# Plain units on whole banks: 512 tokens past each weight tile, four banks instead of three

## The chip, the cores and the metric

One Trainium2 chip, one of its cores. The metric is the device time of one execution in microseconds, the median over several runs; lower is better. The kernel before runs in 2796.94 us (three runs, 2796.71 to 2799.17).

## What is computed

One layer of a hybrid block over 512 tokens of 2048 features, in float32, followed by a final RMSNorm. Cut to what matters here:

```python
h = rmsnorm(x, norm1_w)
proj = h @ w_in                               # [512, 2048] x [2048, 22592]
q, k, v, g_ret, z, xbc, dt_raw, gate_r, gate_s = split(proj)
y_r = retention(q, k, v, positions) * silu(g_ret)          # 8 heads of 256
y_s = rmsnorm(ssd(xbc, dt_raw, ...) * silu(z), ssd_norm_w) # 4096 wide
merged = sigmoid(gate_r) * (y_r @ w_br_ret) + sigmoid(gate_s) * (y_s @ w_br_ssd)
out = rmsnorm(x + merged @ w_out, norm_f_w)
```

Nearly all of the arithmetic is in products of a weight matrix with 2048 features of 512 tokens: 88 blocks of 256 weight columns of `w_in`, 8 of `w_br_ret`, 16 of `w_br_ssd` (two halves of its 4096 rows) and 8 of `w_out`.

## The kernel before, in words

**Units.** `unit` (line 239) makes W^T A for 256 columns of weights and all 512 tokens, feature-major, as two tiles of 128 x 512. It goes through 2048 features in eight pairs of 128-row tiles (`k` in `products`, line 207). Operands of a matmul are F32R, which rounds, so that each product is three matmuls on a high and a low part of either side: high x high (L202), high x low (L203) and low x high (L204), each accumulated in the same place of a PSUM bank. A bank holds 512 float32 a partition, and every matmul here streams 256 of them: one half of the tokens or of a combination of such halves.

**Two recipes.** A pair of weight tiles times a pair of activation tiles is a 2 x 2 block product, with the token halves as the second dimension. `SEVEN` (line 92) is Strassen's product in Winograd's form: seven products of combinations, four banks, 7 x 3 = 21 matmuls for a `k`. `EIGHT` (line 95), for units called with `plain=True`, is the usual eight products on the weights as they are, 24 matmuls for a `k`, in three banks; it spares VectorE the combining of weights (lines 219 to 222) and makes four weight slots instead of seven to split (line 226). The activations are kept once for both recipes, as seven slots of 256 tokens for each `k` and part (`hh`, `hl`; `operands`, line 162), among them A11 (slot 1), A22 (2), A12 (3) and the difference A21 - A11 (6). There is no slot with A21 itself in it. So `EIGHT` puts the products with A11 into bank 0 for both halves of the outputs and adds those with A21 - A11 into banks 1 and 2.

**Which units are plain.** 18 of the 119 units: V and K of head 0, the first x unit of each of the 8 SSD groups (`PLAIN_X`), the last gate unit, units 0 and 7 of each of the three branch projections and unit 0 of the output projection (`PLAIN2`). The last 256 output columns are a case of their own (`PASSES`, line 99), which the change leaves alone. Three of the 18, the units 7 of the branch projections, take their banks from the `att` pool (`alt`); the other 15 have the `acc` banks `pb0` to `pb2`, which have one buffer each, so that the next unit writes a bank only when it has been read out.

**Order in a unit.** For the first five `k` all products of a `k` follow each other; the last three (`LAST`) are taken group by group (lines 234 to 237), so that a bank is complete, and can be read out, while the later groups still run. In `EIGHT` the groups of the last three `k` are 18, 27 and 27 matmuls long.

**Reading out.** A plain unit's banks are read by three instructions (lines 250 to 253): ScalarE copies bank 0 twice over (for each output column tile once) into the 128 x 1024 result `o`, and VectorE adds bank 1 to one half of `o` and bank 2 to the other.

**Weights.** SP issues the loads of raw weights `wf` (line 216), two `k` in a buffer, three buffers; VectorE combines them for `SEVEN`; ScalarE rounds them to `whi` (line 150, seven buffers) and VectorE subtracts for `wlo` (line 151, six buffers). At the start of a stage the same two lines, with lines 155 to 160 on VectorE and POOL, make the operands `hh` and `hl` of the new stage's activations from DRAM. These have one buffer each, so that they wait for the last matmuls of the stage before.

**Order of issue.** The tile framework puts every engine's instructions in an order by priority and by a timing model of its own (`schedule_with_timeline_sim`, line 819); weight preparation and reading out have a raised priority. Some stretches (stage 0, the end) are pinned to the order of the text by `InOrder`, so that their instructions all have line 120.

Of the kernel before, what the change touches and what calls it, by code (L numbers as in the profile page):

```python
# [8 lines left out]
F32 = mybir.dt.float32  # L9
# [3 lines left out]
ALU = mybir.AluOpType  # L13
PSUM = bass.MemoryType.PSUM
DRAM = bass.MemoryType.DRAM
# [16 lines left out]

# columns of the constant array
C_ID, C_TRI, C_ONE, C_FREQ, C_END = 0, 128, 256, 384, 386


def _parts_of_inverse_two_pi():
    """1/(2 pi) as a sum of 12-bit pieces, high to low."""
    digits = 0.15915494309189533576888376337251436203445964574045644874766734405889
    from fractions import Fraction  # L40

    # 1/(2 pi) to 200 bits by Machin's formula
    def atan_inv(n, bits):
        one = 1 << bits
        term = one // n
        total, k, sign = term, 1, 1
        while term:
            term //= n * n
            k += 2
            sign = -sign  # L50
            total += sign * (term // k)
        return total

    bits = 240
    pi = 4 * (4 * atan_inv(5, bits) - atan_inv(239, bits))
    inv = Fraction(1 << bits, 2 * pi)
    assert abs(float(inv) - digits) < 1e-15
    parts = []
    for i in range(5):
        step = Fraction(1, 1 << (14 + 12 * i))  # L60
        n = inv // step
        parts.append(float(n * step))
        inv -= n * step
    return parts


def constants():
# [7 lines left out]
    for h in range(NH):  # L75
# [5 lines left out]

# A 256-row by 256-column block of weights B times a 256-feature by 512-token block of
# activations A.  Rows of A are the token halves, its columns the two feature tiles; t1 is
# half 1 and t0 is half 2, the odd weight tile is column 1 and the even one column 2.
# Activation slots: 0 A21, then A12-(A21+A22-A11), 1 A11, 2 A22, 3 A12, 4 A21+A22,
# 5 A21+A22-A11, 6 A21-A11.
# Weight slots: 0 B12, then B22+B11-B12, 1 B11, 2 B22, 3 B21, 4 B11-B12, 5 B22-B12,
# 6 B21-(B22+B11-B12).
# A product is (bank, half of the bank, weight slot, activation slot).
# SEVEN: Strassen's products in Winograd's form.  EIGHT: the block product with A21 as  # L90
# A11+(A21-A11), on the weights as they are.
SEVEN = (((0, 0, 1, 1), (1, 0, 3, 3), (1, 1, 0, 5)),
         ((2, 0, 5, 6), (2, 1, 4, 4)),
         ((3, 0, 6, 2), (3, 1, 2, 0)))
EIGHT = (((0, 0, 1, 1), (0, 1, 0, 1)),
         ((1, 0, 1, 6), (1, 0, 3, 2), (1, 1, 3, 3)),
         ((2, 0, 0, 6), (2, 0, 2, 2), (2, 1, 2, 3)))
# EIGHT in two passes, the second half of the tokens first, each with banks of its own.
PASSES = ((((0, 0, 1, 1), (0, 1, 0, 1)), ((1, 0, 3, 3), (1, 1, 2, 3))),
# [12 lines left out]
class InOrder:  # L112
    """An engine whose instructions issue in the order of the program."""

# [15 lines left out]
def hybrid_block(tc, A, out):  # L130
# [15 lines left out]
    def att_tile():  # L146
        return att.tile([P, T], F32, name="att")
# [4 lines left out]

    # ------------------------------------------------ products with the weights
    def combined(f, eng):
# [7 lines left out]
    def operands(i, f):  # L162
        """The seven activation operands of feature pair i from its raw slots 0-3 in f."""
        combined(f, POOL if i in FORM_POOL else DVE)
# [12 lines left out]
    def load_operands(forms, src, last=None):  # L177
        """Operands of 2048 features of a DRAM array [features, T]; the last pair may be on chip."""
        H = []
# [9 lines left out]
    def products(H, parts, pt, groups, PE=PE, after=None):  # L189
        """The products of groups, for 256 columns of weights, into the banks pt: parts are  # L190
        DRAM arrays [2048, n], side by side."""
        started, ws = set(), []
# [46 lines left out]
    def unit(H, parts, alt=False, plain=False):  # L239
        """W^T A for 256 columns of weights as two tiles [128, T], feature-major."""  # L240
        nb = 3 if plain else 4
        if alt:
            pt = [att_tile().rearrange("p (h t) -> p h t", h=2) for b in range(nb)]
        else:
            pt = [acc.tile([P, 2, 256], F32, name=f"pb{b}") for b in range(nb)]
        products(H, parts, pt, EIGHT if plain else SEVEN)
        o = op.tile([P, 4, 256], F32, name="o")
        with tc.high_priority():
            if plain:
                ACT.copy(o.rearrange("p (c r) t -> p c r t", c=2),  # L250
                         pt[0][:, :, None, :].to_broadcast([P, 2, 2, 256]))
                DVE.tensor_tensor(o[:, 0:2, :], pt[1], o[:, 0:2, :], op=ALU.add)
                DVE.tensor_tensor(o[:, 2:4, :], pt[2], o[:, 2:4, :], op=ALU.add)
            else:
# [8 lines left out]

    # ---------------------------------------------------------------- stage 0
    cc = cst.tile([P, C_END], F32, name="cc")
# [8 lines left out]

    # scratch
    yr_d = dp.tile([D, T], F32, name="yr_d")
# [12 lines left out]
    def inverse_root(dst, ps, y, z, n, DVE=DVE, ACT=ACT):  # L289
        """dst = (ps / n + eps) ** -0.5 for sums in PSUM; a Newton step makes it exact.  # L290
        y, z: room for one tile each."""
        ACT.activation(y, ps, AF.Abs_reciprocal_sqrt, scale=1.0 / n, bias=eps)
# [4 lines left out]

    # forms of the activations before they are split: A8 and B8 serve other ends between
    bg_ctx = ExitStack()
# [15 lines left out]
    with tc.tile_pool(name="st0", bufs=1) as st:  # L315
        def early(tag):
            """Room of an operand that is not yet there."""
            return hp.tile([P, 7 * 256], F32, name=f"e_{tag}", tag=tag)

        # the order of the arithmetic here is that of the text  # L320
        pe, act, dve, pool = (InOrder(tc, e) for e in (PE, ACT, DVE, POOL))
        raw = [early(f"hl{i}")[:, :2 * T].rearrange("p (r t) -> p r t", r=2) for i in range(NP)]
        wdt = early("hh7")[:, :KD * SH].rearrange("p (k c) -> p k c", k=KD)
        for i, x in enumerate(raw):
            SP.dma_start(out=x, in_=rows(A["xT"], i))
            if i == 0:
                SP.dma_start(out=cc, in_=A["consts"])
        # brings the table in ahead
        act.activation(rstd[:, :1], eps, AF.Abs_reciprocal_sqrt)
# [27 lines left out]

        # the normalized activations
        fs, hs, H = {}, {}, []
# [25 lines left out]
    def rotary_tables(positions, x):  # L385
        """cos and sin of the angles, which are rounded as the reference rounds them, then
        counted in turns and reduced exactly; x is room for four tiles."""
        turn, a1, a2, ki = (x[:, i, :] for i in range(4))
# [34 lines left out]
    def step_sizes(v, pool):  # L423
        """dt = softplus(h w + bias), the cumulative decays in blocks of 128 tokens."""
        u, w, s, s2 = (v[:, i, :].rearrange("p (c h) -> p c h", c=TB) for i in range(4))
# [8 lines left out]
        for tb in range(TB):  # L434
            DVE.scalar_tensor_tensor(u[:, tb, :], pt[:, tb * SH:(tb + 1) * SH], rstd[:, tb:tb + 1], dtb,
                                     op0=ALU.mult, op1=ALU.add)
        # softplus: max(u, 0) + log1p(exp(-|u|)), log1p(w) = 2 atanh(w / (2 + w))
        DVE.tensor_scalar(w, u, -1.0, None, op0=ALU.mult)
# [36 lines left out]

    # -------------------------------------------------------------- retention
    with tc.tile_pool(name="ret", bufs=1) as rp:
# [3 lines left out]
        for h in range(NH):  # L481
            # the decays stay where the gate comes later
            dec = sg[:, 0, :]
# [72 lines left out]

    # -------------------------------------------------------------------- SSD
    with tc.tile_pool(name="ssd", bufs=1) as sp:
        # conv taps and bias; D
        cw = sp.tile([P, 48, 5], F32, name="cw")  # L560
# [12 lines left out]
        def conv(x, j, dst):  # L573
            """causal convolution over tokens and SiLU of one feature block."""
            ACT.activation(dst, x, AF.Identity, scale=cw[:, j, 3:4], bias=cw[:, j, 4:5])
# [13 lines left out]
        for g in range(NG):  # L589
# [14 lines left out]
            for jj in range(2):  # L604
# [5 lines left out]
                for e in range(2):  # L610
# [5 lines left out]
                    for i in range(2):  # L616
                        SP.dma_start(out=E[i * 64:(i + 1) * 64, :], in_=E_d[h0 + i, P:].partition_broadcast(64))
                    # x token-major, scaled by dt, and by dt and the decay to the block's end
                    ps = att_tile()
# [21 lines left out]
                    for i in range(2):  # L641
                        # decay from s to l within a block; s > l is zeroed by CB
                        L = sp.tile([P, TB, P], F32, name="L", bufs=2)
# [28 lines left out]

    # --------------------------------------------------- branch projections
    with tc.tile_pool(name="br", bufs=1) as bp:
# [41 lines left out]

    # ----------------------------------------------------- output projection
    with tc.tile_pool(name="fin", bufs=1) as fp:
# [16 lines left out]

        # the last two feature blocks, the odd one first, half of the tokens after the other
        t = xo[NP - 1]
# [85 lines left out]
```

## Time and profile before

| | |
|---|---|
| Time, median of 3 runs | 2796.94 us |
| Span of the profiled execution, first to last instruction | 2798.7 us |
| TensorE (PE) busy | 2738.8 us, 98%, 22236 matmuls |
| Weight loads (PEld) busy | 2680.0 us, 96% |
| VectorE (DVE) busy | 2380.8 us, 85% |
| ScalarE (ACT) busy | 1333.9 us, 48% |
| POOL busy | 254.1 us, 9% |
| Mean granted TensorE clock | 0.993 |
| DMA, mean | 130 GB/s |

The profiled execution has only its span as its own time; it lies 1.8 us above the median of the runs and within their spread (2796.71 to 2799.17). The profile names a helper's line, so that the matmuls of all units stand under L202 to L204, those of `acc` banks with the tile `pb` and those of `att` banks with `att`; weight loads stand beside them as PEld. An instruction's duration on PE reaches over the pipeline and is longer than the distance from one start to the next; it is the distance that tells how fast the engine goes.

### The profile page before, as it was taken

The page shows a single profiled execution, that of the slowest core. Times are in us where ns is not written, and L with a number is a line of the kernel's source. Part 1 is how long each engine was busy: PE and PEld are TensorE (multiplying, and loading weights), DVE is VectorE, ACT ScalarE, POOL GpSimd, SP SyncE. Part 2 cuts the span into 40 slices and gives each one's busy share as a digit, 9 for nine tenths or more (in the row PEclk, how much of TensorE's full clock was granted, in tenths as well). Part 3 has the DMA queues.
Part 4 walks back from the last instruction along what each step waited for, and adds up shares of the span by engine and source line. Part 5 has one row for each costly group of instructions (what it writes and reads, how often), then busy time and mean ns, then how long its engine had stood idle before and what let it go on. Part 6 is the DMA issues. An engine that isn't in the chain of part 4 may idle for free.

```text
span 2798.7 us, 55732 instructions
## 1 busy us (share of the span) xinstructions
PE 2738.8 (98%) x22236; PEld 2680.0 (96%) x22236; DVE 2380.8 (85%) x3746; ACT 1333.9 (48%) x1885; POOL 254.1 (9%) x206
## 2 busy tenths in 40 slices
PE   7999999999999999999999999999999999999898
PEld 4999999999999999999999999999999999999898
DVE  8998888888879888888888888888888798788997
ACT  4434333333345655564655555555553343433443
POOL 4000000000000000000000000000020030111311
PEclk9999999999999999999999999999999999999999
DMA  3333333333333444343443434334455554566634
GB/s 124 106 97 101 102 102 103 110 92 109 102 104 119 127 134 127 108 137 108 127 125 121 135 121 135 104 118 128 124 187 165 167 180 130 166 184 190 220 105 139
DMA packets 344388, 362.69 MB, mean 130 GB/s; under 512 B 25664, under 2 KB 298304, under 8 KB 344128
## 3 DMA queue, kind: packets, MB, share of 16 engines
q1 hardware_dynamic: 323888, 325.32, 38.5%
q10 hardware_dynamic: 20240, 33.82, 3.3%
q8 instruction: 174, 2.85, 0.4%
q14 instruction: 86, 0.70, 0.1%
HBM read 321.56 MB, written 37.49 MB: 128 GB/s over the span
## 4 chain that ended last, share of the span: by engine, by line
PE 82%; DVE 7%; DMA 6%; issue 3%; POOL 1%; ACT 1%; SPq 0%; DVEq 0%; ACTq 0%; POOLq 0%
PE pb L203 22%; PE pb L202 22%; PE pb L204 22%; PE att L204 2%; PE att L202 2%; PE att L203 2%; PE att L651 2%; DVE wlo L151 2%; DMA wf<-in_w_in_dram 2%; PE att L537 1%; PE att L522 1%; DMA wf<-in_w_br_ssd_dram 1%; PE att L655 1%; PE pb L120 1%; PE att L630 1%
## 5 line engine op out<-in xcount | busy, mean ns | idle before, releaser
L203 PE MATMUL pb<-hl,whi 128*128 128x256 f32 x5944 | 1686.5, 285 | 10.8 <-DVE hl L120 6.0
L202 PE MATMUL pb<-hh,whi 128*128 128x256 f32 x5944 | 1685.7, 285 | 6.2 <-ACT hh L150 3.2
L204 PE MATMUL pb<-hh,wlo 128*128 128x256 f32 x5944 | 1673.5, 284 | 3.7 <-DVE wlo L151 3.6
L150 ACT CAST whi<-wf 128x896 fp32r<-128x896 f32 (+1 forms) x968 | 822.1, 885 | 873.9 <-PE pb L203 414.8
L203 PEld LDWEIGHTS pb<-hl,whi 128*128 128x128 f32 x5944 | 1141.9, 192 | 17.6 <-DVE hl L120 6.9
L202 PEld LDWEIGHTS pb<-hh,whi 128*128 128x128 f32 x5944 | 1139.3, 192 | 10.2 <-ACT hh L150 3.6
L204 PEld LDWEIGHTS pb<-hh,wlo 128*128 128x128 f32 x5944 | 1136.0, 192 | 5.5 <-DVE wlo L151 5.1
L151 DVE TENSOR_TENSOR wlo<-wf,whi 128x896 fp32r<-128x896 f32 (+1 forms) x968 | 997.4, 1040 | 78.6 <-PE pb L204 25.9
L219 DVE TENSOR_TENSOR wf<-wf 128x512 f32<-128x512 f32 x404 | 286.3, 709 | 168.1 <-DMA wf<-in_w_in_dram 114.3
L204 PE MATMUL att<-hh,wlo 128*128 128x256 f32 x864 | 241.8, 285 | 7.8 <-DVE wlo L151 7.8
L202 PE MATMUL att<-hh,whi 128*128 128x256 f32 x864 | 245.4, 285 | 1.4 <-ACT whi L150 1.4
L203 PE MATMUL att<-hl,whi 128*128 128x256 f32 x864 | 244.8, 285 | 0.0
L221 DVE TENSOR_TENSOR wf<-wf 128x256 f32<-128x256 f32 x404 | 182.8, 454 | 4.3
L204 PEld LDWEIGHTS att<-hh,wlo 128*128 128x128 f32 x864 | 165.1, 193 | 8.8 <-DVE wlo L151 8.8
L222 DVE TENSOR_TENSOR wf<-wf 128x256 f32<-128x256 f32 x404 | 170.7, 424 | 3.2
L202 PEld LDWEIGHTS att<-hh,whi 128*128 128x128 f32 x864 | 167.6, 194 | 1.8 <-ACT whi L150 1.6
L203 PEld LDWEIGHTS att<-hl,whi 128*128 128x128 f32 x864 | 167.5, 194 | 0.0
L626 POOL TENSOR_TENSOR xl<-xd,sst 128x384 f32<-128x384 f32 x32 | 33.6, 1049 | 876.9 <-DVE xd L623 819.7
L646 ACT ACTIVATE L<-L,sst 128x128 f32<-128x128 f32 x256 | 80.1, 390 | 59.6 <-DMA L<-A_d 47.1
L256 ACT COPY o<-pb 128x256 f32<-128x256 f32 x89 | 32.9, 370 | 144.4 <-PE pb L204 137.2
L257 DVE TENSOR_TENSOR o<-pb,o 128x512 f32<-128x512 f32 x89 | 60.9, 684 | 34.5 <-PE pb L204 34.2
L543 POOL TENSOR_TENSOR rs<-rs,mhalf 128x1 f32<-128x1 f32 x32 | 24.9, 784 | 709.5 <-DVE rs L542 700.2
(230 smaller groups left out, 2113.1 us busy)
## 6 DMA issues: line engine op xcount, KB each, us to landing
wf<-in_w_in_dram SPq DMA_DIRECT2D x640, 256.0 KB, 3.1
wf<-in_w_br_ssd_dram SPq DMA_DIRECT2D x128, 256.0 KB, 3.6
wf<-in_w_out_dram SPq DMA_DIRECT2D x72, 256.0 KB, 3.2
wf<-in_w_in_dram SPq DMA_DIRECT2D x128, 128.0 KB, 2.6
L<-A_d SPq DMA_DIRECT2D x64, 256.0 KB, 3.5
wf<-in_w_br_ret_dram SPq DMA_DIRECT2D x64, 256.0 KB, 3.7
ys_d<-B ACTq DMA_DIRECT2D x32, 256.0 KB, 2.8
E<-E_d SPq DMA_DIRECT2D x64, 96.0 KB, 3.0
```

The costliest lines, as they stand in the source:

```text
L150: ACT.copy(dst_hi, src)
L151: DVE.tensor_tensor(dst_lo, src, dst_hi.bitcast(F32), op=ALU.subtract)
L202: PE.matmul(o, wh, xh, start=b not in started, stop=False, skip_group_check=True)
L203: PE.matmul(o, wh, xl, start=False, stop=False, skip_group_check=True)
L204: PE.matmul(o, wl, xh, start=False, stop=(k == NP - 1), skip_group_check=True)
L219: DVE.tensor_tensor(f2[:, :, 4:6, :], f2[:, :, 1:3, :], f2[:, :, 0:1, :].to_broadcast([P, 2, 2, P]), op=ALU.subtract)
L221: DVE.tensor_tensor(f2[:, :, 0, :], f2[:, :, 2, :], f2[:, :, 4, :], op=ALU.add)
L222: DVE.tensor_tensor(f2[:, :, 6, :], f2[:, :, 3, :], f2[:, :, 0, :], op=ALU.subtract)
L257: DVE.tensor_tensor(o[:, 1:3, :], pt[1], p1[:, None, :].to_broadcast([P, 2, 256]), op=ALU.add)
L626: POOL.tensor_tensor(xl, xd[:, :TB - 1], tail[:, :TB - 1, hs, None].to_broadcast([P, TB - 1, 2, 64]), op=ALU.mult)
L646: ACT.activation(L[:, c, :], L[:, c, :], AF.Relu, scale=-1.0, bias=At[:, c, h0 + i:h0 + i + 1])
L651: PE.matmul(pi[i * 64:(i + 1) * 64, c * P:(c + 1) * P], xd[:, c, i, :], L[:, c, :], start=True, stop=True)
```

## The change

Plain units take their products from `FOUR` instead of `EIGHT`. A product's half and its activation slot are now slices: `ALL` is both halves of a bank, 512 columns, `A1` the slots 1 and 6 (A11 and A21 - A11), `A2` the neighbouring slots 2 and 3 (A22 and A12). Each of the four weight slots meets each of its activations in one matmul of 512 columns, and has a bank to itself: banks 0 and 1 belong to one output column tile, banks 2 and 3 to the other. So a `k` has 12 matmuls of 512 columns instead of 24 of 256, the same columns in all. `unit` takes four banks for both recipes, and reads out for each output column tile in three steps: ScalarE copies the A11 half of the first bank twice, VectorE adds that bank's other half (256 columns) to the second half of the tokens, then the whole second bank (512 columns). `products` is unchanged, except that its text goes without its docstring, and `SEVEN`, `PASSES` and the lists of plain units stay. The other lines of the diff take out comments and docstrings only.

```diff
-EIGHT = (((0, 0, 1, 1), (0, 1, 0, 1)),
-         ((1, 0, 1, 6), (1, 0, 3, 2), (1, 1, 3, 3)),
-         ((2, 0, 0, 6), (2, 0, 2, 2), (2, 1, 2, 3)))
-# EIGHT in two passes, the second half of the tokens first, each with banks of its own.
+ALL, A1, A2 = slice(0, 2), slice(1, 7, 5), slice(2, 4)
+FOUR = (((0, ALL, 1, A1),), ((1, ALL, 3, A2),), ((2, ALL, 0, A1),), ((3, ALL, 2, A2),))
...
     def unit(H, parts, alt=False, plain=False):
-        """W^T A for 256 columns of weights as two tiles [128, T], feature-major."""
-        nb = 3 if plain else 4
+
         if alt:
-            pt = [att_tile().rearrange("p (h t) -> p h t", h=2) for b in range(nb)]
+            pt = [att_tile().rearrange("p (h t) -> p h t", h=2) for b in range(4)]
         else:
-            pt = [acc.tile([P, 2, 256], F32, name=f"pb{b}") for b in range(nb)]
-        products(H, parts, pt, EIGHT if plain else SEVEN)
+            pt = [acc.tile([P, 2, 256], F32, name=f"pb{b}") for b in range(4)]
+        products(H, parts, pt, FOUR if plain else SEVEN)
         o = op.tile([P, 4, 256], F32, name="o")
         with tc.high_priority():
             if plain:
-                ACT.copy(o.rearrange("p (c r) t -> p c r t", c=2),
-                         pt[0][:, :, None, :].to_broadcast([P, 2, 2, 256]))
-                DVE.tensor_tensor(o[:, 0:2, :], pt[1], o[:, 0:2, :], op=ALU.add)
-                DVE.tensor_tensor(o[:, 2:4, :], pt[2], o[:, 2:4, :], op=ALU.add)
+                for c in range(2):
+                    ACT.copy(o[:, 2 * c:2 * c + 2, :], pt[2 * c][:, 0:1, :].to_broadcast([P, 2, 256]))
+                    DVE.tensor_tensor(o[:, 2 * c, :], pt[2 * c][:, 1, :], o[:, 2 * c, :], op=ALU.add)
+                    DVE.tensor_tensor(o[:, 2 * c:2 * c + 2, :], pt[2 * c + 1], o[:, 2 * c:2 * c + 2, :], op=ALU.add)
```

## Rows read from the trace of the kernel before

**Rows 1.** The page's busy time, share of the span, instructions of each engine.

```profile
PE 2738.8 (98%) x22236; PEld 2680.0 (96%) x22236; DVE 2380.8 (85%) x3746; ACT 1333.9 (48%) x1885; POOL 254.1 (9%) x206
```

**Rows 2.** PE timeline inside a plain x unit: start us, us, instruction.

```profile
1276.75 0.28 PE L202 MATMUL pb<-hh,whi 128*128 128x256 f32 x1
1276.87 0.28 PE L203 MATMUL pb<-hl,whi 128*128 128x256 f32 x1
...
1278.31 0.28 PE L203 MATMUL pb<-hl,whi 128*128 128x256 f32 x1
```

**Rows 3.** PE timeline in a stretch of lower clock, start of the first branch projection.

```profile
2096.72 0.42 PE L202 MATMUL att<-hh,whi 128*128 128x256 f32 x1
...
2097.79 0.41 PE L203 MATMUL att<-hl,whi 128*128 128x256 f32 x1
```

**Rows 4.** Stretches: us, PE, PEld, DVE, ACT, POOL busy (instructions), PEclk, DMA share, GB/s.

```profile
2096.10:2100.00 3.90, 3.88 (x19) 3.87 (x20) 3.90 (x4) 2.41 (x2) 2.36 (x1) 0.56 0.41 124
43.00:76.00 33.00, 26.85 (x195) 25.74 (x196) 31.00 (x31) 15.00 (x14) 19.07 (x13) 0.90 0.15 43
76.00:808.00 732.00, 732.00 (x5826) 714.74 (x5826) 623.58 (x1088) 284.44 (x367) 24.91 (x32) 1.00 0.34 102
808.00:2058.00 1250.00, 1245.52 (x10386) 1229.52 (x10385) 1063.54 (x1688) 707.88 (x1113) 78.03 (x63) 1.00 0.41 123
2081.60:2109.00 27.40, 25.43 (x195) 24.81 (x194) 25.38 (x34) 12.82 (x14) 9.86 (x8) 0.94 0.58 173
2605.00:2640.00 35.00, 26.62 (x204) 26.01 (x203) 32.05 (x42) 16.98 (x18) 12.62 (x10) 0.90 0.41 125
```

**Rows 5.** PE timeline before the first unit: float32 matmuls of 512 and 2 columns.

```profile
40.77 1.45 PE L120 MATMUL att<-e_hl,e_hh 128*64 128x512 f32 x3
42.16 1.05 PE L120 MATMUL att<-cc,R 128*128 128x2 f32 x8
43.07 0.36 PE L202 MATMUL pb<-hh,whi 128*128 128x256 f32 x1
```

**Rows 6.** Who PE waited for, 76 to 2058 us: us in total, times, longest.

```profile
PE att L595 <- ACT A L580: 2.0, 1, 2.0
PE pb L202 <- DVE o L257: 1.0, 1, 1.0
PE pb L204 <- DVE wlo L151: 0.2, 1, 0.2
```

**Rows 7.** The same from 2058 us to the end.

```profile
PE att L204 <- DVE wlo L151: 7.8, 5, 3.3
PE pb L203 <- DVE hl L151: 4.7, 2, 4.5
PE pb L204 <- DVE wlo L151: 3.5, 4, 1.1
PE pb L202 <- ACT hh L150: 3.2, 2, 2.9
```

**Rows 8.** Reading out, by line and shape: busy us, mean ns, idle before and why.

```profile
L250 ACT COPY o<-pb 128x1024 f32<-128x1024 f32 x15 | 15.2, 1014 | 22.0 <-PE pb L204 22.0
L250 ACT COPY o<-att 128x1024 f32<-128x1024 f32 x3 | 3.0, 1001 | 0.0
L252 DVE TENSOR_TENSOR o<-pb,o 128x512 f32<-128x512 f32 x15 | 10.3, 687 | 13.0 <-PE pb L204 13.0
L253 DVE TENSOR_TENSOR o<-pb,o 128x512 f32<-128x512 f32 x15 | 10.2, 682 | 0.0
L259 DVE TENSOR_TENSOR o<-o,pb 128x256 f32<-128x256 f32 x89 | 36.6, 412 | 0.0
L510 ACT ACTIVATE A<-o 128x512 f32<-128x512 f32 x16 | 9.3, 626 | 3.8 <-DVE o L260 3.7
```

**Rows 9.** Who DVE waited for, whole span: us in total, times, longest.

```profile
DVE o L252 <- PE pb L204: 13.0, 10, 2.1
```

## The prediction, made blind

> **What bounds the kernel now.** I read the busy shares first. TensorE is busy for 98% of the span, its weight loads for 96%, VectorE for 85% [rows 1]. A PE duration reaches over the pipeline, so a high share does not yet tell the bound; the list of what PE waited for does. From 76 to 2058 us, over two thirds of the time, its waits come to a handful of microseconds [rows 6]: there the time is the number of matmuls times the distance between two starts. After 2058 us the branch and output projections have real waits, for weights and operands that VectorE and ScalarE make [rows 7]; the first unit of the program waits too, with VectorE busy 31.0 of 33.0 us [rows 4]. So a faster unit pays in full in the middle, and may be taken back by VectorE where a stage begins.
>
> The distance itself is in the timeline. Inside a plain unit 14 matmuls of 256 columns start within 1.56 us, 0.120 us apart [rows 2], at granted clock 1.00, the 2.4 GHz level. 256 columns at one a cycle would take 0.1067. Where the clock was granted at half, after PE had stood idle at the start of a stage, six starts lie 1.07 us apart, 0.214 each [rows 3, 4], and 256 columns at 1.2 GHz are 0.2133. So a column costs one cycle and hardly anything is fixed beside it; yet at full clock 13 ns come from elsewhere. Eight matmuls of 2 columns each take 0.91 us until the next kind starts, 0.114 each [rows 5]: about that is the least that a matmul with a weight load of its own takes, however little it streams. I read the 0.120 as this floor, in sight because 256 columns at full clock are shorter than a load.
>
> **The change part by part.** *Matmuls.* A plain unit has 8 x 24 = 192 matmuls of 256 columns, 192 x 0.120 = 23.04 us. It gets 96 of 512 columns. No row shows such a matmul in F32R. The lower bound is one column a cycle, 0.213; the upper, if the 13 ns stay on every matmul, 0.227, and 0.240 if they belong to the columns. The nearest row for a long stream is the float32 one: three of 512 columns last 1.45 us together, and with 0.59 for the last one's pipeline that is 0.43 from start to start [rows 5], or 2 cycles a column (0.4267) and some 3 ns. I take 0.216, because the half-clock stretch, whose stream is also longer than the load, shows neither 13 ns more (0.227) nor an eighth more (0.240). A unit then takes 96 x 0.216 = 20.74 us, 2.30 less; 18 units (15 and 3 copies of bank 0 [rows 8]), 41.5 us.
>
> The Trainium skill (TensorE: Matmul & The Clock Gate, section Back-to-back issue gap) gives for a single stream N/2.4 + 2.5 ns, 109 ns for 256 columns and 216 for 512. By it a pair of matmuls would win 2.6 ns instead of 24, and the whole change 1728 x 2.6 ns = 4.5 us instead of 41.5. The trace disagrees at 256 columns (120), and so I go by the row.
>
> *Where it counts.* Thirteen of the 18 units stand where PE has next to no wait behind it: K of head 0 (in 76 to 808 us, PE busy throughout), the eight x units and the last gate unit (808 to 2058 us and just beyond), and units 7 of the three branch projections, the last of their stages. These give 13 x 2.30 = 29.9 us. VectorE has the room for it in the long middle stretch: 1063.5 us busy of 1250 [rows 4], 85%, and 1070 of 1232 afterwards, 87%. The other five are the first of a stage: V of head 0 and units 0 of the four projections. In two of them PE is busy for 26.85 of 33 us and 26.62 of 35, VectorE for 31.0 and 32.1 [rows 4]; PE gets operands as VectorE finishes them, and a shorter stream waits longer for the same operand. I count them at nothing; the bounds are 0 and 11.5 us.
>
> *Reading out.* Now ScalarE copies once, 1.01 us, and VectorE adds twice, 0.687 + 0.682 [rows 8]. Afterwards ScalarE copies 512 columns twice, 0.63 each by the nearest 512-column row, 0.24 more a unit at 48% load: nothing. VectorE adds 256 and 512 columns, twice: 2 x (0.412 + 0.682) = 2.19 us, 0.82 more a unit. In the middle stretch the 15% that VectorE is idle hide it. At the four changes of stage from 2058 us on it does not: the last unit's adds stand in VectorE's queue with the operands for which PE is about to wait. I charge 4 x 0.82 = 3.3 us; the bounds are 0 and 14.8 for all 18.
>
> *The fourth bank.* A plain unit first writes bank 3 after 9 matmuls, 1.9 us; the unit before needs one add of 0.68 for it after its own end. The next seven-product unit writes bank 3 after 15 x 0.120 = 1.8 us, against 9 x 0.120 = 1.1 us for bank 2 now, which was the plain unit's last. Neither is tight, and waits for a bank are now single ones of up to 1.0 us [rows 6]: nothing either way. No DMA is added or moved; SP's queue only meets a consumer that is 10% faster in 18 of 119 units.
>
> *Order.* The tile framework works out every engine's order from its own times, which the change alters. No row prices that; I take nothing, and some 6 us to either side.
>
> The sum: 29.9 - 3.3 = 26.6 us. The profiled execution's span of 2798.7 becomes 2772.1; the median lies 1.8 below that span, so 2796.9 becomes **2770.3 us**.
>
> **The rivals.**
> *All 18 units pay.* Operands of a new stage are rounded into buffers that the old stage's last matmuls release, and those come earlier; if VectorE starts that much earlier and the adds hide, it is 41.5 us: 2755.4. For it: at the branch stages PE also finds work in a neighbouring unit while it waits (the matmuls into `att` banks at 2096 us [rows 3] belong to the second unit, while the first, in `pb` banks, is not yet through). Against: VectorE's 32.1 of 35 us at the last change of stage.
> *The 13 ns stay on each matmul.* Then 1.28 us a unit: 13 x 1.28 - 3.3 = 13.3 us, 2783.6. Against it stands the half-clock distance of 0.214.
> *Stage ends are taken back too.* If VectorE or the transfers pace a new stage from before the old one's end, the gate unit and the three units 7 give nothing: 9 x 2.30 - 3.3 = 17.4 us, and longer waits bring another stretch or two of half clock, some 1.5 us each (16 matmuls at 0.214 instead of 0.120): 2782.5. For it: waits of up to 4.5 us [rows 7].
> *Nothing to win in the stream.* The 0.120 is what 256 F32R columns cost at full clock, load or no load; 512 take 0.240, PE gains nothing, and VectorE's 3.3 us are left: 2800.2, no change that can be told. For it: no row has a longer F32R stream. Against: an eighth more per column would make 0.240 of 256 columns at half clock, where the row has 0.214. The skill's rule for the gap, above, ends near this case by another way, at 2792.4.
> *VectorE's queue blocks, and the kernel is slower.* VectorE takes its instructions in order. An add that waits for a bank holds up the weight splits behind it; it did so 10 times before the first add of a plain unit, 13.0 us in all [rows 9]. The new reading out has four adds and more places to wait. If PE then waits for `wlo` once a plain unit as long as the longest such wait now, 3.3 us [rows 7], it is 18 x 3.3 = 59.4 against 29.9: 2826. It decides from 1.7 us a unit (29.9 / 18). Against: in the middle PE waited 0.2 us for `wlo` in all [rows 6], so the splits run well ahead, and a wait there must first eat that lead.
>
> **How the numbers follow.** Forecast 0.58; all units 0.10; 13 ns stay 0.10; stage ends 0.10; nothing 0.04; slower 0.08. The first four are gains beyond 0.2% (5.6 us, about what a measurement of this kernel can tell from no change): faster 0.88, same 0.04, slower 0.08. The range holds these four: from the full 41.5 us with 2 to spare, 2753, to the two weaker ones at 2783.6 with as much, 2786. Its bounds also take in the unknown order (6 us) around the forecast.
>
> **What would show it.** PE should have 20508 matmuls (3456 fewer of 256 columns, 1728 of 512), starts in a plain unit 0.216 us apart, and a plain x unit of 96 x 0.216. From 76 to 2058 us the waits should stay at some microseconds, with VectorE at 87%; the waits after 2058 us and before 76 us should grow by several microseconds, as the five units' 11.5 us turn into waiting. The forecast is wrong in its main term if the distance is 0.227 or 0.240, in its second if the waits at the changes of stage grow by much more than 11 us, and as a whole if waits for `wlo` show up in the SSD stretch behind the x units.

## The result and the profile after

The median goes from 2796.8 us (4 runs of the kernel before, 2794.8 to 2799.2) to 2780.3 us (4 runs, 2777.5 to 2781.3): a ratio of 0.9935, with the interval 0.9921 to 0.9949. Timed anew, beside other kernels, it was 0.9928 (0.9915 to 0.994). In the rest of this text a gain is (1 - ratio) x 2797 us, so 18.2 us here and 20.1 us the second time, where 26.6 were forecast. The sign and the range hold; the size does not. The profiled execution has a span of 2777.6 us, 21.1 less than before.

The page's line of busy time, beside [rows 1]:

```profile
PE 2715.8 (98%) x20508; PEld 2586.4 (93%) x20508; DVE 2391.4 (86%) x3782; ACT 1336.1 (48%) x1905; POOL 253.1 (9%) x206
```

PE has the 20508 matmuls foretold, and the 1728 spared take only 23.0 us off its busy time. The PE timeline in a plain x unit (start us, us, instruction), beside [rows 2], says why:

```profile
1277.65 0.39 PE L204 MATMUL pb<-hh,wlo 128*128 128x512 f32 x1
...
1280.83 0.39 PE L203 MATMUL pb<-hl,whi 128*128 128x512 f32 x1
```

From the first row to the last are 14 distances in 3.18 us, 0.227 each. Of the three prices that the prediction had named for a matmul of 512 columns (0.213 to 0.216, 0.227, 0.240) it is the middle one: twice the 0.1067 of 256 columns, and 13 to 14 ns once for each matmul. A unit saves 96 x 13.3 ns = 1.28 us and not 2.30.

The first matmuls of this x unit, of the unit after it and of the x unit of the next SSD group, before:

```profile
1272.07 0.28 PE L202 MATMUL pb<-hh,whi 128*128 128x256 f32 x1
...
1296.43 0.28 PE L202 MATMUL pb<-hh,whi 128*128 128x256 f32 x1
...
1432.59 0.28 PE L202 MATMUL pb<-hh,whi 128*128 128x256 f32 x1
```

and after:

```profile
1274.45 0.40 PE L202 MATMUL pb<-hh,whi 128*128 128x512 f32 x1
...
1297.64 0.28 PE L202 MATMUL pb<-hh,whi 128*128 128x256 f32 x1
...
1433.09 0.40 PE L202 MATMUL pb<-hh,whi 128*128 128x512 f32 x1
```

The x unit takes 23.19 us, where before it took 24.36: 1.17 less. The whole group takes 158.64 us, where it took 160.52: 1.88 less. The 0.71 us that the x unit does not explain are taken up with `banks_only` below.

The stretches beside [rows 4] (us, then busy of PE, PEld, DVE, ACT, POOL, PEclk, DMA share, GB/s):

```profile
43.00:76.00 33.00, 23.67 (x84) 17.96 (x83) 30.99 (x31) 14.25 (x13) 18.75 (x12) 0.86 0.16 44
808.00:2040.00 1232.00, 1227.50 (x9583) 1183.30 (x9582) 1063.69 (x1699) 707.47 (x1120) 78.91 (x62) 1.00 0.41 125
70.10:76.90 6.80, 5.63 (x13) 4.46 (x14) 6.66 (x8) 2.13 (x2) 0.00 (x0) 0.50 0.54 147
```

In the SSD stretch VectorE works 1063.69 of 1232 us, 86% (87% were foretold), and PE is still busy throughout. From the first matmul of the first x unit to that of the last gate unit it takes 1235.9 us, where it took 1250.1: 14.2 us of the 21.1 come from here. The two matmuls, before and then after:

```profile
808.45 0.28 PE L202 MATMUL pb<-hh,whi 128*128 128x256 f32 x1
...
2058.56 0.28 PE L202 MATMUL pb<-hh,whi 128*128 128x256 f32 x1
```

```profile
810.88 0.40 PE L202 MATMUL pb<-hh,whi 128*128 128x512 f32 x1
...
2046.80 0.40 PE L202 MATMUL pb<-hh,whi 128*128 128x512 f32 x1
```

The first of the eight x units does not gain: it takes 28.8 us, where it took 26.6. PE waits longer for ScalarE in it (3.2 us, where [rows 6] have 2.0), and after this wait the clock is granted at half for 3.4 us, which it was not before. The granted clock of that place (the third number from the right), before and after:

```profile
820.00:840.00 20.00, 18.54 (x156) 18.55 (x157) 15.48 (x23) 11.64 (x15) 0.00 (x0) 1.00 0.23 69
820.00:840.00 20.00, 16.47 (x73) 13.46 (x72) 12.55 (x22) 14.65 (x19) 0.00 (x0) 0.91 0.18 53
```

In the first unit of the program VectorE has no room, 30.99 of 33 us. The second unit starts at 78.6 us, where before it started at 76.0: 2.6 us later, though the first began 1.2 us earlier (41.9 for 43.1), so that from start to start it is 36.7 us for 32.9.

PE's waits from 76 to 2046 us (us in total, times, longest), beside [rows 6]:

```profile
PE att L599 <- ACT A L579: 3.2, 1, 3.2
PE att L654 <- DVE S L636: 0.7, 2, 0.4
PE pb L204 <- DVE wlo L151: 0.3, 1, 0.3
```

and from 2046 us to the end, beside [rows 7]:

```profile
PE pb L202 <- ACT hh L150: 7.1, 2, 6.0
PE pb L204 <- DVE wlo L151: 5.6, 3, 3.3
PE pb L203 <- DVE hl L151: 2.5, 3, 1.2
PE att L204 <- DVE wlo L151: 2.0, 4, 1.3
```

In the middle PE waits 0.3 us for `wlo` in all, so the rival in which VectorE's queue blocks did not come about. All waits after 2046 us together are 22.3 us, and were 22.7: at the changes of stage they moved from one name to another, but did not grow. From 43 to 80 us they did, from 6.2 to 9.3 us, now all for `hl`, which VectorE makes:

```profile
PE pb L203 <- DVE hl L120: 9.3, 4, 3.2
```

Reading out, by line and shape (busy us, mean ns, idle before and why), beside [rows 8]:

```profile
L252 DVE TENSOR_TENSOR o<-pb,o 128x512 f32<-128x512 f32 x30 | 20.5, 685 | 0.0
L251 DVE TENSOR_TENSOR o<-pb,o 128x256 f32<-128x256 f32 x30 | 12.5, 418 | 1.2 <-ACT o L250 1.2
L250 ACT COPY o<-pb 128x512 f32<-128x512 f32 x30 | 17.3, 584 | 36.6 <-PE pb L204 36.6
```

2 x (0.418 + 0.685) = 2.21 us of VectorE a unit, where 2.19 were worked out. The waits of the first add for a bank, 13.0 us before [rows 9], are gone: it is ScalarE's copy that waits for the unit's end now, 36.6 us in the last row where it was 22.0, on an engine that is busy for less than half of the time.

### The profile page after: what moved, and what is told of

Its sections match the earlier page's. It is cut to its first block, busy times and chain, and to the rows that moved or that the text cites. A ratio compares the mean times of both kernels' runs of the same rounds, so it can differ in the third digit from the quotient of the medians.

```text
span 2777.6 us, 52322 instructions
## 1 busy us (share of the span) xinstructions
PE 2715.8 (98%) x20508; PEld 2586.4 (93%) x20508; DVE 2391.4 (86%) x3782; ACT 1336.1 (48%) x1905; POOL 253.1 (9%) x206
## 4 chain that ended last, share of the span: by engine, by line
PE 82%; DVE 8%; DMA 5%; issue 3%; ACT 1%; POOL 1%; SPq 0%; DVEq 0%; POOLq 0%; ACTq 0%
PE pb L204 23%; PE pb L203 23%; PE pb L202 23%; PE att L202 2%; PE att L204 2%; PE att L203 2%; DVE wlo L151 2%; PE att L650 2%; DMA wf<-in_w_in_dram 1%; PE att L536 1%; PE att L521 1%; DMA wf<-in_w_br_ssd_dram 1%; DVE hl L151 1%; PE pb L120 1%; PE att L654 1%
## 5 line engine op out<-in xcount | busy, mean ns | idle before, releaser
L203 PE MATMUL pb<-hl,whi 128*128 128x256 f32 (+1 forms) x5464 | 1601.1, 294 | 11.9 <-DVE hl L120 9.3
L202 PE MATMUL pb<-hh,whi 128*128 128x256 f32 (+1 forms) x5464 | 1596.8, 295 | 9.9 <-ACT hh L150 7.1
L204 PE MATMUL pb<-hh,wlo 128*128 128x256 f32 (+1 forms) x5464 | 1587.9, 294 | 6.0 <-DVE wlo L151 6.0
L203 PEld LDWEIGHTS pb<-hl,whi 128*128 128x128 f32 x5464 | 1049.1, 192 | 34.6 <-DVE hl L120 11.0
L202 PEld LDWEIGHTS pb<-hh,whi 128*128 128x128 f32 x5464 | 1046.4, 192 | 33.8 <-ACT hh L150 8.4
L204 PEld LDWEIGHTS pb<-hh,wlo 128*128 128x128 f32 x5464 | 1041.0, 192 | 28.1 <-DVE wlo L151 6.8
L202 PE MATMUL att<-hh,whi 128*128 128x256 f32 (+1 forms) x768 | 227.0, 297 | 1.4 <-ACT whi L150 1.4
L203 PE MATMUL att<-hl,whi 128*128 128x256 f32 (+1 forms) x768 | 226.7, 297 | 0.0
L204 PE MATMUL att<-hh,wlo 128*128 128x256 f32 (+1 forms) x768 | 222.7, 297 | 2.0 <-DVE wlo L151 2.0
L204 PEld LDWEIGHTS att<-hh,wlo 128*128 128x128 f32 x768 | 144.8, 191 | 7.0 <-DVE wlo L151 2.8
L203 PEld LDWEIGHTS att<-hl,whi 128*128 128x128 f32 x768 | 147.5, 192 | 3.9
```

The lines of the kernel that those rows point to most:

```text
L202: PE.matmul(o, wh, xh, start=b not in started, stop=False, skip_group_check=True)
L203: PE.matmul(o, wh, xl, start=False, stop=False, skip_group_check=True)
L204: PE.matmul(o, wl, xh, start=False, stop=(k == NP - 1), skip_group_check=True)
```

## The experiments

**Where do the 13 ns sit?** `stream` is a kernel of matmuls alone, 48 of a kind behind each other.

```diff
+for i in range(48):
+    PE.matmul(b0, wr[:, i % 4, :], xr[:, 2:4, :], ...)    # 512, slots together
+for i in range(48):
+    PE.matmul(b0, wr[:, i % 4, :], xr[:, 1:7:5, :], ...)  # 512, slots 1 and 6
...
```

> Computes none of the block: only 14 streams of matmuls one after the other on one core, each on a line of its own, 48 long (24 for float32), so that the distance between two starts can be read for each kind. Theory A, a fixed price: every F32R matmul at full clock costs its columns at 2.4 GHz plus 13 ns, whatever it reads and writes: 512 columns 0.227 us (runs of columns together or apart, one bank or four, one weight tile or four, 64 or 128 weight columns), 384 columns 0.173, 256 columns 0.120; bfloat16 without the 13 ns, 0.109 at 256 and 0.216 at 512; float32 passes 0.429 at 512. Theory B, the weights: the 13 ns belong to handing over 128 F32R weight columns, so that 64 weight columns show some 6 ns less (0.220 at 512) and one weight tile for all may show none. Theory C, the pattern of the change: columns together in one bank cost 0.216, and the 11 ns come with columns that lie apart, or with going from bank to bank.

Measured: its timeline of PE (start us, us, engine, line, operation, tiles, shape, count), from the second of its 14 stretches to the last but one:

```profile
22.22 11.04 PE L174 MATMUL bk<-xr,wr 128*128 128x512 f32 x48
33.10 11.04 PE L177 MATMUL bk<-xr,wr 128*128 128x512 f32 x48
43.98 11.04 PE L179 MATMUL bk<-xr,wr 128*128 128x512 f32 x48
54.86 11.04 PE L182 MATMUL bk<-xr,wr 128*128 128x512 f32 x48
65.73 11.20 PE L185 MATMUL bk<-xr,wr 128*64 128x512 f32 x48
76.78 8.51 PE L188 MATMUL bk<-xr,wr 128*128 128x384 f32 x48
85.12 5.91 PE L191 MATMUL bk<-xr,wr 128*128 128x256 f32 x48
90.87 5.61 PE L194 MATMUL bk<-xr,wr 128*64 128x256 f32 x48
96.32 10.53 PE L197 MATMUL bk<-xb,wb 128*128 128x512 bf16 x48
106.69 5.40 PE L200 MATMUL bk<-xb,wb 128*128 128x256 bf16 x48
111.93 20.77 PE L203 MATMUL bk<-raw,rw 128*128 128x512 f32 x48
132.53 10.52 PE L206 MATMUL bk<-raw,rw 128*128 128x256 f32 x48
```

A start less the start before it, over 48, is the distance: (33.10 - 22.22) / 48 = 0.227 with the slots together (L174), the same with slots 1 and 6 (L177), with four banks in turn (L179) and with one weight tile throughout (L182), where each matmul still has a load of its own. 384 columns (L188) take 0.174, 256 (L191) 0.120. At 0.41667 ns a column that leaves 13.3, 13.8 and 13.1 ns: a fixed amount for each F32R matmul, whatever its length. The same shapes in bfloat16 (L197, L200) take 0.216 and 0.109, 2.7 and 2.5 ns over the columns; float32 (L203, L206) has 48 records for 24 calls, so two passes a call, of 0.429 and 0.216 (the next stretch begins at 142.89), 2.5 ns over two cycles a column. The Trainium skill (TensorE: Matmul & The Clock Gate, section Back-to-back issue gap) has N/2.4 + 2.5 ns; the bfloat16 rows agree with it to some tenths of a nanosecond, the F32R rows do not.

So the floor of weight loads, on which the prediction rested, is not where the 0.120 comes from: 384 and 512 columns (0.160 and 0.213 by themselves) are longer than the 0.114 that was read as a load, and have the 13 ns all the same. With 64 weight columns the distance of 256 columns falls to 0.1135 (L194), but that of 512 does not fall (0.230, L185); so neither theory A, which had 0.120 and 0.227 there, nor theory B, which had 0.220 for the longer one, holds as it stands. Theory C does not hold: together or apart, one bank or four, it is 0.227. What in the engine takes the 13 ns, and why for F32R alone, these rows do not tell; a price of handing over the weights is not excluded.

**Order, bank and reading out without the long matmul.** `banks_only` is the change with every matmul of 512 columns cut back into two of 256:

```diff
-FOUR = (((0, ALL, 1, A1),), ((1, ALL, 3, A2),), ((2, ALL, 0, A1),), ((3, ALL, 2, A2),))
+FOUR = (((0, 0, 1, 1), (0, 1, 1, 6)), ((1, 0, 3, 2), (1, 1, 3, 3)), ((2, 0, 0, 1), (2, 1, 0, 6)), ((3, 0, 2, 2), (3, 1, 2, 3)))
```

> The new four banks and the new reading out in all 18 plain units, but matmuls of 256 columns (24 a k, as before). Theory A (the gain is the 13 ns of 1728 matmuls that are no longer there, 23 us on PE): nothing is gained here, 2797 us, up to 2800 with VectorE's 0.8 us more a unit on the path. Rival (a good part of the gain comes from the fourth bank, the shorter groups or the order that they bring): 2785 to 2790.

Measured: 0.9987 (0.9978 to 0.9996), 3.6 us faster than before, though it pays the new reading out in full; that is between the two expectations. Between this kernel and the change lie the long matmuls alone: 18.2 - 3.6 = 14.6 us, by the second timing 20.1 - 3.6 = 16.5. Were all 1728 spared matmuls worth 13.3 ns, it would be 23.0; were it 13 units, 16.6.

Where the 3.6 us come from is seen in the matmuls of one line in the SSD stretch, the decays `L` times the inputs `xd` (busy us, mean ns). Before and after:

```profile
L651 PE MATMUL att<-L,xd 128*64 128x128 f32 x512 | 59.5, 279 | 0.4 <-DVE L L649 0.4
```

```profile
L650 PE MATMUL att<-L,xd 128*64 128x128 f32 x512 | 54.7, 279 | 0.0
```

The same 512 matmuls of the same mean, but 4.8 us less of PE. In `banks_only`:

```profile
L650 PE MATMUL att<-L,xd 128*64 128x128 f32 x512 | 54.8, 279 | 0.0
```

The timeline shows how. Before, the 16 matmuls of one pair of heads in a group stand in two blocks of 8, with units' matmuls between:

```profile
1335.38 1.09 PE L651 MATMUL att<-L,xd 128*64 128x128 f32 x8
1336.39 0.39 PE L203 MATMUL pb<-hl,whi 128*128 128x256 f32 x1
1336.62 0.28 PE L204 MATMUL pb<-hh,wlo 128*128 128x256 f32 x1
...
1337.17 1.09 PE L651 MATMUL att<-L,xd 128*64 128x128 f32 x8
```

After, as one block:

```profile
1338.31 0.28 PE L203 MATMUL pb<-hl,whi 128*128 128x256 f32 x1
1338.52 1.58 PE L650 MATMUL att<-L,xd 128*64 128x128 f32 x16
1340.03 0.49 PE L654 MATMUL att<-A,S 128*128 128x128 f32 x2
```

Sixteen together take 1.51 us to the next start (1340.03 - 1338.52), and twice eight 2 x (1336.39 - 1335.38) = 2.02. Each block moreover costs 0.1 at its beginning (0.21 from the unit's last start to the block's first, not 0.12) and 0.1 at its end (0.23 for the unit's first matmul after it): 0.7 us for each pair joined, once in each of the 8 groups, 5.6 us. Counted over the whole trace, of the 32 blocks of 16 that there can be 17 stand together before, 25 in the change and in `banks_only`. The SSD stretch of `banks_only` is 5.9 us shorter than before, and the group that was set side by side above takes 159.82 us in it:

```profile
1279.17 0.28 PE L202 MATMUL pb<-hh,whi 128*128 128x256 f32 x1
...
1438.99 0.28 PE L202 MATMUL pb<-hh,whi 128*128 128x256 f32 x1
```

So in a group the two causes come apart: 160.52 less 159.82 is the joined pair (0.70), and 159.82 less 158.64 the long matmuls of one x unit (1.18). The joining comes with the framework's order; by what reckoning that came out so is open.

**The x units alone, and all but them.** Both keep the old recipe beside the new and choose it by call:

```diff
-    def unit(H, parts, alt=False, plain=False):
+    def unit(H, parts, alt=False, plain=False, old=False):
...
-        products(H, parts, pt, FOUR if plain else SEVEN)
+        products(H, parts, pt, EIGHT if old else FOUR if plain else SEVEN)
```

`x_only` gives `old=True` to all plain units but the eight x units, `not_x` to those eight alone.

> The new recipe in the 8 x units of the SSD stage alone, the old one in the other ten plain units. If units in the middle keep their 96 x 13.3 ns = 1.28 us each: 2796.8 - 10.2 = 2786.6 us. If the order that the framework makes costs or gives several us there: outside 2783 to 2790.

> The new recipe in the ten plain units outside the SSD groups, the old one in the 8 x units. If the parts add up (the x units alone gave as much as the whole change): within 3 us of the kernel before. If each unit keeps its 1.28 us wherever it stands: 12.8 us below the kernel before.

Measured: `x_only` 0.9936 (0.9922 to 0.995), 17.9 us; `not_x` 0.9975 (0.9964 to 0.9986), 7.0 us. The eight x units would be 8 x 1.28 = 10.2 us by their matmuls; with the 5.6 us of order 15.8, so `x_only` lies outside the 2783 to 2790 us that its expectation had for no effect of order. The order goes with the x units: 25 blocks stand together in `x_only`, and in `not_x` the decay matmuls are as before the change, 17 together.

```profile
L659 PE MATMUL att<-L,xd 128*64 128x128 f32 x512 | 59.5, 279 | 0.2 <-DVE L L657 0.2
```

The ten others give 7.0; five that count would be 5 x 1.28 = 6.4, ten 12.8; neither expectation, 3 us or 12.8, is met. The two parts make 24.9 us where the whole has 18.2 to 20.1; with intervals of 3 to 4 us to either side of each number that is no contradiction, and no proof of a loss in their meeting either.

**The first unit.** In the trace of after, PE waits 3.24 us for `hl` in the first unit, and goes on at half clock, the 1.2 GHz level (timeline of PE):

```profile
71.27 0.79 PE L203 MATMUL pb<-hl,whi 128*128 128x512 f32 x1 [3.24 <-DVE hl L120]
71.86 0.63 PE L204 MATMUL pb<-hh,wlo 128*128 128x512 f32 x1
...
73.14 0.63 PE L203 MATMUL pb<-hl,whi 128*128 128x512 f32 x1
```

Three distances from 71.86 take 1.28 us, 0.427 each, which is 512 columns at 1.2 GHz and nothing beside them: the 13 ns are there at full clock only. Is this unit better off with the old recipe? `v0_old` gives `old=True` to it alone:

> The new recipe in all plain units but the first of the program (V of head 0), which has the old one. In the trace of the change this unit is through 2.6 us later than before, though it has less to stream, and VectorE stands further ahead with the weights of the next unit. If that loss is the order which the new recipe brings VectorE there, the old recipe gives it back: 2780.3 - 2.6 = 2777 to 2778 us. If the loss is made up later anyway, or comes from elsewhere: 2780 to 2782.

Measured: 0.9914 (0.9901 to 0.9928), 24.1 us, and 2772.8 us where the change had 2780.3 in runs of another time. That looked like 6 us in this one unit, more than it had lost, and three kernels ask for the cause. `v0_fill` puts 50 matmuls of 256 columns, whose result nobody reads, between its products so that PE does not stand idle:

```diff
+                if fill is not None and k >= 2:
+                    for i in range(10):
+                        PE.matmul(fill[:, 0, :], ws[k][0][:, 1, :], H[k][0][:, 1, :], start=(i == 0), stop=(i == 9),
+                                  skip_group_check=True)
...
```

> The change, with 50 matmuls of 256 columns more in the first unit (V of head 0): ten after each of five feature pairs, where PE waits for the next operand, into a bank that nobody reads. They add 6.0 us of work to some 9 us of waiting. Theory D (the first unit loses time because PE, through sooner with each pair, stands idle longer, and the clock is granted at half after it, while the rest of the unit runs): with PE kept at work the clock stays at 1.00, and the next unit starts some 3 us earlier than with the change: 2777 us, though there is more to do. Rival (VectorE's order there, or the operands themselves): the added work brings nothing, 2780 to 2783, or comes on top, 2786.

Measured: 0.995 (0.9937 to 0.9964), 14.0 us. The stretch of half clock was still there, and the fillers fell into it; this decides nothing. `v0_last1` lets all products of a `k` follow each other up to the seventh, so that PE has more to do when an `hl` comes:

```diff
-            if k < NP - LAST:
+            if k < NP - last:
...
-                for i, x in enumerate(unit(H, cols(VO), plain=h in PLAIN_V)):
+                for i, x in enumerate(unit(H, cols(VO), plain=h in PLAIN_V, last=LAST if h else 1)):
```

> The change, with the first unit's products taken feature pair by feature pair up to the seventh and only the last pair bank by bank (elsewhere the last three). After the last operand 12 matmuls of 512 columns are left, 2.7 us, instead of 30 (6.8 us). If what is left after the last operand sets the unit's end, at half clock or not, the next unit starts 4 us or more earlier: 2775 to 2776. Rival (the four banks then end at nearly the same time, and the next unit waits for their reading out): 2779 to 2781.

Measured: 0.9943 (0.993 to 0.9955), 15.9 us; the second unit starts as late as in the change. `v0_256` cuts that unit's matmuls into 256 columns, as in `banks_only`, on four banks:

> The change, with V of head 0 on the new four banks and the new reading out, but in matmuls of 256 columns. Theory D (the shorter stream makes PE wait longer there, and the clock falls): as the old recipe in that unit, 3 to 8 us below the change. Rival (the four banks, the reading out or the order that they bring cost the time there): no faster than the change, within 2 us of it.

Measured: 0.9939 (0.9926 to 0.9951), 17.1 us, no faster than the change. Its second unit starts 38.3 us after the first, and that of `banks_only`, which has the same matmuls there, 38.4; PE waits 2.8 and 1.6 us before that start, until an add of the reading out has freed a bank. With the old recipe, the same 192 matmuls on three banks, it is 32.9 to 35.6 us in six traces. So what makes this unit late is not that its matmuls are longer: it comes with the four banks, the reading out or the order, as the rival in the expectation says. Then the change and `v0_old` were timed anew on one chip with `v0_256` and `not_x`.

> The change as it is, once more, so that the next three stand beside it on one chip. 2778 to 2782 us, or the same ratio, 0.9935.

> The change with the old recipe in V of head 0, once more. If its lead over the change is the first unit's and not the scatter of one afternoon: 3 to 8 us below the change of this call. If it was scatter: within 2 us of it.

Measured: the change 0.9928 (2775.9 us, 2771.9 to 2777.8), `v0_old` 0.9921 (0.9909 to 0.9934; 2774.5 us). They are 1.4 us apart with intervals of some 3.5 us to either side of each: most of the first lead was scatter. In this second trace of the change the half clock lay elsewhere, 66.0 to 69.4 us, so where it falls is a matter of the execution:

```profile
66.00:69.40 3.40, 3.40 (x10) 2.42 (x8) 3.40 (x6) 1.04 (x1) 1.16 (x1) 0.50 0.08 19
70.10:76.90 6.80, 5.12 (x20) 3.60 (x20) 6.80 (x9) 3.73 (x5) 0.00 (x0) 1.00 0.51 145
```

From the first unit's start to the second's it is 36.7 and 35.6 us in these two traces, and 35.1 in `not_x`, which has the new recipe there too; with the old one the six traces spread from 32.9 to 35.6, with 33.9 and 35.5 for `v0_old` alone. A price of 1 to 2 us for the first unit is thus likely, but not shown: the spread of one and the same kernel is as large. How much of it is waits and how much the clock stays open.

**The firsts of a stage.** `first_old` gives `old=True` to the first unit and to units 0 of the four projections; `v0x0_old` to the first unit and the first x unit, in which the change waits 3.2 us for ScalarE.

> The old recipe in the five units that are the first of a stage (V of head 0, units 0 of the four projections), the new one in the other 13. If the first units give nothing or lose, as the prediction counted them: no slower than with V alone on the old recipe, 2770 to 2774. If they keep their 1.28 us each: 4 x 1.28 = 5.1 us above it, 2778.

> The old recipe in V of head 0 and in the first x unit of the first SSD group, the new one in the other 16. That x unit is 1.7 to 3.9 us later through in the traces of the three kernels that have the new recipe there, with a wait of 3.2 us for ScalarE's SiLU of the group's C. If the recipe brings that wait: 2772.8 - 2 to 4 = 2769 to 2771. If the wait is of that place whatever the recipe: 2773 to 2775.

Measured: `first_old` 0.9935 (0.9922 to 0.9947), 18.2 us; `v0x0_old` 0.9924 (0.9912 to 0.9937), 21.3 us. Beside the change (18.2, 20.1) the five firsts give nothing that can be told. Beside `v0_old` (24.1, 22.1) `first_old` lacks 4 to 6 us, and four units 0 at 1.28 us would be 5.1. Both would fit if the first unit cost some 2.6 and the units 0 of the projections gave some 5: the net, 2.5 us, is inside the intervals. But the traces do not bear the 5 us out: from the last gate unit to the end `first_old` takes 731.2 us, and nine traces with the new recipe in all these units 728.3 to 732.8. So these runs do not settle the firsts one by one. For the first x unit the times tell nothing, but the traces do: it takes 26.1 to 26.6 us in the three that have the old recipe there (before, `not_x`, `v0x0_old`) and 28.0 to 30.9 in the ten with the four banks; each of the ten, and none of the three, has a stretch of half clock in it, of 3.4 or 6.8 us. With the four banks it is 1.4 us or more longer, where it was to be 1.28 shorter. No version is clearly ahead of the change.

## Why the prediction was right and wrong

**Right: the place.** The unit's matmuls pay in the middle, where PE has no waits behind it: 1.17 us, of 1.28, in seven of the eight x units. The first x unit was one of the thirteen that were counted, and loses 2.1 us, by its longer wait and the half clock after it. Not all 18 pay: the change less `banks_only` is 14.6 and 16.5 us, some 5 to either side, near 13 units (16.6) and short of 18 (23.0). That the five firsts give nothing together fits `first_old`; that each gives nothing isn't shown. VectorE's longer reading out was costed rightly (2.21 for 2.19 us), the fourth bank costs nothing that shows in the middle, though it may in the first unit (`v0_256`), and no queue blocks.

**Wrong: the price of a matmul of 512 columns.** "I take 0.216, because the half-clock stretch [...] shows neither 13 ns more (0.227) nor an eighth more (0.240)." The matmul takes 0.227, which the prediction had named as the sign that its main term is wrong. The half-clock rows [rows 3] were read rightly, but they hold for half clock alone: F32R has its 13 ns at full clock and none at half, in the change too (0.227 and 0.427). The two-column matmuls of [rows 5], at 0.114, were taken for the floor that explained the 0.120; they were near it by accident, since the same 13 ns stand behind 384 and 512 columns. The term was to be 13 x 2.30 = 29.9 us; at the price found it is 13 x 1.28 = 16.6.

The rival "the 13 ns stay on each matmul" is what happened, and it had 0.10. Its 2783.6 is above both medians (2780.3 and 2775.9), for two reasons.

**Too low: the order, put at nothing with some 6 us to either side.** Joining the decay matmuls of a pair of heads gives 5.6 us, within those bounds. The sum now: 12 x 1.28 = 15.4 and 5.6, less 2.1 at the first x unit and 2.6 at the first unit in the profiled executions, 16.3 us, where 18.2 and 20.1 were measured. Stretch by stretch it does not close. The SSD stretch should by it be 7 x 1.17 + 5.6 - 2.1 = 11.7 us shorter, and is 14.2 (16.9 in the second trace of the change); the rest lies in single units that are longer than their like in other groups, by 5.0 us in all before and 2.3 after; before, PE waits in them mostly for a bank [rows 6]. What follows should be shorter by the last gate unit and the three units 7, 4 x 1.28 = 5.1 us, and is by 9.3. But there the profiled execution of `x_only`, whose units are the old ones from the last gate unit on, is 4.9 us shorter too, and that of `banks_only`, with no long matmul, 9.6, so that single executions can't tell what the change does in that place.

**Too high: the charge of 3.3 us at the changes of stage.** The waits there are 22.3 us against 22.7, and `banks_only`, which has the charge without the long matmuls, is faster than before. The longer adds do not hold up the next operands by anything that shows. That the forecast is only 6 to 8 us beside the measured gain is luck in part: the price was 13.3 us too high, the order and this charge together some 9 too low.

**Also wrong: that the firsts' 11.5 us would turn into waiting.** At the changes of stage the waits did not grow; in the first unit they did, by 3.1 us. With 1.28 us a unit there was less to turn into waiting, and whether units 0 of the projections keep theirs can't be told at this size.

## What to carry to other kernels

A distance at a reduced clock does not tell what is fixed beside the columns at full clock: measure the very shape and type that a change brings, in a stream by itself, before it is priced. For F32R on 128 weight columns the win of twice as many columns in half as many matmuls was 13 ns here for each matmul spared, where PE had no other wait. A new shape in a few units also re-orders the rest of the kernel, here by several microseconds, so set beside a change a version that has its order and not its gain, and time it more than once before you hunt a difference of 6 us.

## What was not expected of the hardware

- F32R on 128 x 128 weights: 0.120, 0.174 and 0.227 us for 256, 384 and 512 columns at full clock, so 13 to 14 ns fixed a matmul; 0.214 and 0.427 at half clock for 256 and 512, with nothing fixed. bfloat16: 2.5 to 2.7 ns.
- With 64 weight columns the 256-column distance is 0.1135, the 512-column one 0.230 and not below 0.227.
- A block of short matmuls among the units' has a cost for each block: 0.51 us in the distance for 8 and 8 instead of 16, and 0.1 at either edge.
